# Six of the seven down products on scaled fp16 halves instead of fp32r halves

## The chip, the cores and the metric

The kernel runs on one core of one Trainium2 chip. The metric is the device time of one execution in microseconds (us). The five engines are TensorE (PE; its weight loads are listed apart as PEld), VectorE (DVE), ScalarE (ACT), GpSimd (POOL) and SyncE (SP, which here only issues DMAs).

## What is computed

Two layers of an encoder on 1024 tokens of width 1024. Each layer has an attention and a convolution branch, an output product, and a gated feed-forward block. The change lies in the second half of that block. Cut to it, the reference is:

```python
h2 = _rmsnorm(x, g_ffn[l])
z = _dwconv(h2 @ w_up[l], w_dw_ffn[l], b_dw_ffn[l])     # 1024 -> 2 * 2816, three taps along the tokens
zg, zv = jnp.split(z, 2, axis=-1)
x = x + (jax.nn.silu(zg) * zv) @ w_down[l]              # 2816 -> 1024, the "down" product
```

All inputs and the output are fp32. w_down has 22 blocks of 128 rows per layer.

## The kernel before

**Split operands.** TensorE multiplies fp32 numbers as a sum of two parts, hi and lo. ScalarE writes hi (a rounding copy), VectorE writes lo (source minus hi), and each product of two tiles is three matmuls: hi*hi, hi*lo, lo*hi. In the up products the parts are fp16, of operands first scaled by a power of two (`upper`, `lower`, lines 1183 to 1187; ScalarE adds the squares of each weight block, line 1130, one small matmul with ones sums them over the partitions, line 1163, and a few tiny VectorE operations make the exponent, lines 1132 to 1140). In the down products the parts are fp32r, unscaled (`pair`, lines 1616 to 1622).

**Seven products.** Up and down products are done by Strassen's scheme on two by two blocks: seven half-size products instead of eight. In the down stage (`down_steps`, line 1355) the halves are those of the 22 row blocks (j and j + 11), of the tokens (`done` = 0:512, `rest` = 512:1024) and of the output columns. The seven products run in `ORDER` = 1, 5, 6, 3, 7, 2, 4. Each has 11 steps j, a step is four output tiles m by three matmuls (`product`, line 1420), so 12 matmuls of 128x128 by 128x512. The sums of weight blocks that the scheme wants for products 5, 6, 3 and 7 are made during the up stage (`sum_load`, `sum_step`, `sum_store`, lines 1276 to 1288) and kept in DRAM; products 1, 2 and 4 read w_down itself. Sums of activations are made by VectorE in place (`combine`, line 1400). Eight PSUM banks form two sets of four: products 1, 6, 7, 4 accumulate in set 0 one on top of the other, 5 and 3 in set 1, 2 again in set 1. After each product VectorE adds the bank into x (`evict`, line 1444).

**The order of work.** `feed` (line 926) makes a list of TensorE steps: the output product, 154 up steps, 77 down steps. `put(step, rank, f)` hangs everything else behind a step; within a step, ranks decide. Each engine then runs its own instructions in exactly this order, and semaphores join the engines. For down step n: the weight rows are fetched by SP at n - 8 (`fetch`, pairs of j, into the three "wr" slots) and split at n - 4 (`turn`); `combine` stands at n - 3 (products 5, 6, 7), `pair`, the split of the activations, at n - 2 (eight "m" slots); evictions stand at the next product's first step. Products 2 and 4 (`DOWN_ADDED`) get their weights in another way: GpSimd's DMA queue loads and rounds hi (`cast`, line 1383), ScalarE writes its negative, and a second, adding DMA makes lo (`complete`, line 198).

**Ends.** In layer 0 the last three j of product 4 are done tile by tile (m outermost). In layer 1 it is the last six, and there in two column halves (`ENDS`): 144 matmuls of 128x256 in eight steps of 18, between which the final normalisation starts (lines 1557 to 1566).

**Around it.** Block f of the activations is finished by `close` (line 1264) in the up stage; blocks below 18 are stored to DRAM (`act_store`) and loaded back, 18 to 21 stay in SBUF. The 31 slots tagged "b" hold 128x1024 tiles of all kinds.

Of the kernel before, what the change touches and what calls it, by code (L numbers as in the profile page):

```python
# [9 lines left out]
F32 = mybir.dt.float32  # L10
# [21 lines left out]
NF = DFF // 128  # L32
# [103 lines left out]
class Encoder:  # L136
# [959 lines left out]
    def up_steps(self, l, steps, put):  # L1096
# [5 lines left out]
        self.kept = {}  # L1102
        raw, wts, zs, st, sums, scale, back, nback = defaultdict(dict), {}, defaultdict(dict), {}, {}, {}, {}, {}
        sub = lambda o, p, q, op=ALU.subtract: nc.vector.tensor_tensor(out=o, in0=p, in1=q, op=op)

# [158 lines left out]
        def close(f):  # L1264
# [5 lines left out]
            st["act", f] = z["v"]  # L1270

        def act_store(f):
            if f < KEPT:
                nc.sync.dma_start(out=self.actd[l][f], in_=st.pop(("act", f)))

        def sum_load(j):
            sums[j] = [self.blk(f"sd{l}_{j}{e}") for e in range(2)]
            for e, t in enumerate(sums[j]):
                nc.sync.dma_start(out=t, in_=a["w_down"][l, j + e * (NF // 2)])

        def sum_step(j, n):
# [73 lines left out]
    def down_steps(self, l, steps, put):  # L1355
        nc, a = self.nc, self.a
        base, last, half = len(steps), l == DEPTH - 1, NF // 2
        done, rest = HALVES
        act, x, casts, w, pairs, ps, nxt, sq, late_r, turns = {}, {}, {}, {}, {}, {}, {}, {}, {}, {}
        sub = lambda o, p, q, op=ALU.subtract: nc.vector.tensor_tensor(out=o, in0=p, in1=q, op=op)  # L1360
        spare = lambda name: self.pp.tile([128, 512], F32, name=name, tag="d4", bufs=1)
        other = lambda name: self.pp.tile([128, 512], F32, name=name, tag="d5", bufs=1)
# [19 lines left out]

        def cast(i, j):
            casts[i, j] = self.cast_pair(source(i, j, 1)[:, 0], f"wd{l}_{i}{j}", "wr" if j % 4 == 3 else "ws")

        def fetch(i, j):
            n = min(2, half - j)
            t = self.tmp("wr", f"wd{l}_{i}{j}r", F32, (128, 2, 512))
            nc.sync.dma_start(out=t[:, 0:n], in_=source(i, j, n))
            for k in range(n):  # L1390
                casts[i, j + k] = t[:, k]
# [21 lines left out]
        def pair(i, j):  # L1413
            src = {1: (j, rest), 5: (j, rest), 6: (j, rest), 3: (half + j, done), 7: (j, done), 2: (half + j, rest),
                   4: (half + j, rest)}[i]
            pairs[i, j] = self.pair(act[src[0]][:, src[1]], f"ab{l}_{i}{j}", "b" if i == 4 else "m")
            if i == 4:
# [16 lines left out]
        def evict_end(c, m):  # L1434
            xm = x[4 + m][:, ENDS[c]]
            sub(xm, xm, ps[BANK_SET[4], m][:, cols[c]])
            sq[c, m] = self.blk(f"xsq{l}_e{c}{m}")[:, 0:256]
# [16 lines left out]
        for i, j in order:  # L1454
# [10 lines left out]
            late = max(0, j - tail - 3) if i == 4 else 0  # L1465
            if i in DOWN_ADDED:
                put(need - 7 + late, 5, lambda i=i, j=j: cast(i, j))
            elif j % 2 == 0:
                put(need - 8, 5, lambda i=i, j=j: fetch(i, j))
            put(need - 4 + late - late // 2, 4, lambda i=i, j=j: turn(i, j))  # L1470
            if i in (5, 6, 7):
                put(need - 3, 3, lambda i=i, j=j: combine(i, j))
            put(need - 2, 3, lambda i=i, j=j: pair(i, j))
            if i == 2:
                put(need - 1, 3.5, lambda j=j: combine(4, j))
        for m in range(3, 4 if not last else 3):
            steps.append(lambda m=m: [product(4, j, (m,)) for j in range(tail, half)])
# [586 lines left out]
```

## Time and profile before

| | us |
|---|---|
| median of three runs | 2242.82 (2242.24 to 2243.37) |
| the profiled execution, its own time | 2243.32 |
| its span, first to last instruction | 2241.4 |
| TensorE busy in the span | 2228.5 |
| VectorE, ScalarE, GpSimd busy | 1806.3, 1360.0, 655.3 |
| up products, first to last start, layer 0 | 506.2 to 908 |
| down products, first to last start, layer 0 | 908.6 to 1119 |
| down products, first to last start, layer 1 | 2018 to 2231.6 |

Views of the profile used below: the page; groups of instructions by line and shape (busy time, mean ns of one, idle time before and what ended it); the timeline of an engine (start, length, line, output and input, count of merged instructions, idle time before in brackets). Neighbouring instructions of an engine overlap in part, so the distance of two starts is often a little less than the length of one.

### The profile page before, as it was taken

To read this page: it belongs to the slowest core of one execution; us is meant where nothing else is said; L and a number is where in the kernel's file an instruction comes from. 1 tells how busy PE (TensorE), PEld (TensorE's weight loads), DVE (VectorE), ACT (ScalarE), POOL (GpSimd) and SP (SyncE) were. 2 spreads that over 40 slices of the span, in tenths; PEclk is the share of its full clock that TensorE was granted. 3 is DMA by queue.
4 is the path that set the end of the run, shared out by engine and by line. 5 is a ranking of instruction groups with operands and counts; after the bars stand their busy time and mean duration, and the time that the engine had idled before them with its cause. 6 is when DMAs were issued, how large, how long until landed. Compare 5 with 4: busy or idle time off the path is not lost.

```text
span 2241.4 us, 30140 instructions
## 1 busy us (share of the span) xinstructions
PE 2228.5 (99%) x10762; PEld 1511.7 (67%) x10762; DVE 1806.3 (81%) x2484; ACT 1360.0 (61%) x2078; POOL 655.3 (29%) x631
## 2 busy tenths in 40 slices
PE   9999999999999999999999999999999999999998
PEld 8887777784444444788888877777744444448887
DVE  6989888768998887876559798887798988878765
ACT  5355977745766666544533568776467666655444
POOL 1222788511121111002412237964111121110032
PEclk9999999999999999999999999999999999999999
DMA  6888988955589896646968999979645888856466
GB/s 192 166 181 274 198 188 183 275 139 120 130 230 266 220 261 149 209 156 196 207 140 168 206 265 203 189 164 245 165 104 135 252 261 226 248 154 234 143 150 170
DMA packets 176965, 434.80 MB, mean 194 GB/s; under 512 B 24768, under 2 KB 32816, under 8 KB 176816
## 3 DMA queue, kind: packets, MB, share of 16 engines
q0 software_dynamic: 79520, 176.31, 41.4%
q1 hardware_dynamic: 97008, 256.04, 34.0%
q8 instruction: 85, 1.39, 0.3%
q10 hardware_dynamic: 288, 0.53, 0.1%
q14 instruction: 64, 0.52, 0.1%
HBM read 293.56 MB, written 80.40 MB: 167 GB/s over the span
## 4 chain that ended last, share of the span: by engine, by line
PE 94%; DMA 3%; DVE 1%; ACT 1%; issue 0%; SPq 0%; POOL 0%; DVEq 0%; POOLq 0%; ACTq 0%
PE p L1223 36%; PE pd L1426 19%; PE po L958 7%; PE s L1686 7%; PE o L1749 4%; PE t L1726 4%; PE pq L236 3%; PE pa L236 3%; PE pkv L236 2%; PE pg L236 2%; PE pg L554 2%; DMA wo<-in_w_o 1%; PE pk L236 1%; PE pa L554 1%; PE pn L236 1%; PE pv L1662 1%
## 5 line engine op out<-in xcount | busy, mean ns | idle before, releaser
L1223 PE MATMUL p<-b,w 128*128 128x512 f16 x3696 | 803.6, 379 | 0.0
L1223 PEld LDWEIGHTS <-w 128*128 128x128 f16 x3696 | 361.7, 99 | 426.9 <-DVE w L1187 0.6
L1426 PE MATMUL pd<-ab,wd 128*128 128x512 f32 (+1 forms) x1920 | 422.7, 382 | 0.0
L1426 PEld LDWEIGHTS pd<-ab,wd 128*128 128x128 f32 x1920 | 350.7, 188 | 69.7 <-DVE ab L1621 0.4
L1114 POOL DMA_DIRECT2D wu<-in_w_up x176 | 152.8, 882 | 745.4 <-DVE w L1187 520.7
L1686 PE MATMUL s<-k,q 96*128 96x512 f32 x768 | 207.7, 406 | 1.0 <-DVE qn L750 1.0
L1729 DVE SCALAR_TENSOR_TENSOR pt<-t,pt 128x512 f16<-128x512 f32 x256 | 164.8, 684 | 40.5 <-ACT pt L1728 39.9
L1187 DVE SCALAR_TENSOR_TENSOR w<-wu,wf,w 128x512 f16<-128x512 f32 (+1 forms) x216 | 177.0, 833 | 4.0 <-ACT w L1184 4.0
L1728 ACT ACTIVATE pt<-t 128x512 f16<-128x512 f32 x256 | 139.2, 596 | 57.6 <-PE t L1726 56.6
L1918 POOL TENSOR_TENSOR late<-gate,par 128x1016 f32<-128x1016 f32 (+11 forms) x78 | 168.9, 2166 | 13.8 <-PE pn L236 13.8
L1184 ACT ACTIVATE w<-wu,wf 128x512 f16<-128x512 f32 (+1 forms) x216 | 162.0, 781 | 0.2 <-DMA wu<-in_w_up 0.2
L1688 DVE TENSOR_REDUCE mx<-s 128x1 f32<-128x1024 f32 x128 | 155.6, 1216 | 0.0
L1686 PEld LDWEIGHTS s<-k,q 96*128 96x128 f32 x768 | 135.2, 189 | 23.9 <-DVE qn L750 1.4
L1901 DVE SCALAR_TENSOR_TENSOR conv<-gate,par,conv 128x1009 f32<-128x1009 f32 (+7 forms) x112 | 142.3, 1274 | 3.7 <-ACT conv L616 1.0
L1696 ACT ACTIVATE p<-s,mx 128x1024 f32<-128x1024 f32 x128 | 143.4, 1120 | 2.1 <-DVE mx L1688 1.7
L1619 ACT CAST ab<-ac 128x512 fp32r<-128x512 f32 x130 | 80.0, 616 | 102.5 <-DVE ac L1360 65.1
L1726 PEld LDWEIGHTS t<-ident,p 128*128 128x128 f32 x1024 | 119.7, 141 | 25.9 <-ACT p L1696 0.8
L1627 ACT ACTIVATE o<-zg,par 128x1024 f32<-128x1024 f32 x44 | 54.5, 1238 | 135.1 <-DVE zg L1231 135.1
L1726 PE MATMUL t<-ident,p 128*128 128x128 f32 x1024 | 133.7, 273 | 0.4 <-ACT p L1696 0.2
L1749 PE MATMUL o<-pt,v 128*128 128x512 f16 x512 | 132.5, 381 | 1.2 <-DVE pt L1729 1.1
L920 POOL DMA_DIRECT2D wd<-in_w_down x44 | 32.9, 751 | 322.2 <-PE pd L1426 321.2
L1633 DVE SCALAR_TENSOR_TENSOR o<-zg,par,o 128x1023 f32<-128x1023 f32 x88 | 112.6, 1280 | 8.0 <-ACT o L1627 6.5
(2114 smaller groups left out, 3871.4 us busy)
## 6 DMA issues: line engine op xcount, KB each, us to landing
wu<-in_w_up SPq DMA_DIRECT2D x98, 512.0 KB, 4.8
wu<-in_w_up POOLq DMA_DIRECT2D x176, 256.0 KB, 4.8
sd<-in_w_down SPq DMA_DIRECT2D x44, 512.0 KB, 5.0
ws<-sd SPq DMA_DIRECT2D x44, 512.0 KB, 8.1
wd<-in_w_down POOLq DMA_DIRECT2D x88, 256.0 KB, 5.6
act<-v SPq DMA_DIRECT2D x36, 512.0 KB, 7.3
ac<-act SPq DMA_DIRECT2D x72, 256.0 KB, 5.0
wo<-in_w_o POOLq DMA_DIRECT2D x64, 256.0 KB, 7.6
```

What stands on the lines that cost most here:

```text
L236: nc.tensor.matmul(ps[:, HALVES[c]], w, x[:, HALVES[c]], start=(k == 0 and s == 0), stop=(k == n - 1 and s == 2))
L958: self.nc.tensor.matmul(ps, p[:, sl], q[:, cs], start=(k == 0 and t == 0), stop=(k == 3 and t == 2))
L1184: nc.scalar.activation(out=t, in_=src, func=AF.Copy, scale=scale[f])
L1187: nc.vector.scalar_tensor_tensor(out=t, in0=src, scalar=scale[f], in1=hi, op0=ALU.mult, op1=ALU.subtract)
L1223: nc.tensor.matmul(ps, w[p][:, k * 128:(k + 1) * 128], b[:, q], start=(i in (1, 5, 2) and k == 0 and t == 0), stop=(k == 3 and t == 2), sk ...
L1426: nc.tensor.matmul(ps[t, m][:, cs], w[i, j][p][:, m * 128:(m + 1) * 128], b[:, q, cs], start=(i in (1, 5, 2) and j == 0 and s == 0), stop= ...
L1686: nc.tensor.matmul(ps[:, cs], q[i][0:96, qs], k[j][0:96, cs], start=(s == 0), stop=(s == 2))
L1688: nc.vector.tensor_reduce(out=mx, in_=ps, op=ALU.max, axis=AX.X, negate=True)
L1726: nc.tensor.transpose(tp[:, i, qi * 128:(qi + 1) * 128], st["p"][2 * qp + qi][:, kt * 128:(kt + 1) * 128], self.ident)
L1729: nc.vector.scalar_tensor_tensor(out=lo, in0=tp, scalar=P_SCALE, in1=hi, op0=ALU.mult, op1=ALU.subtract)
L1749: nc.tensor.matmul(po, v[2 * c + i][:, h // 2, e, :], pt[s][:, 2 * (c % 2) + i, :], start=(c == 0 and i == 0 and s == 0), stop=(c == 3 and ...
L1918: self.nc.gpsimd.tensor_tensor(out=p[:, lo:hi], in0=u[:, lo + s:hi + s], in1=self.tap(l, j, t).broadcast_to([128, hi - lo]), op=ALU.mult)
```

## The change

The first product (i = 1) stays as it was. The other six use fp16 parts of scaled operands, with one scale for all activations and one for all w_down of a layer.

- The scales come from sums of squares: 22 ScalarE squares of the closed activation blocks and 22 of the w_down blocks, all in the up stage; one matmul with ones behind down step 6; eight tiny VectorE operations (`scales`).
- Weights of products 2 and 4 are now fetched raw by SP as those of the others; `cast` and `complete` go out of the down stage. For the six products `turn` splits the rows of two j at once.
- Evictions multiply by the inverse scale. Set 0 holds product 1 unscaled when product 6 adds to it, so its four banks are multiplied in place (`rescale`).
- The loads for the weight sums come one step earlier; four activation stores come later; the last pairs of layer 1 come up to three steps earlier.

```diff
+SQUARE_LAG = {0: 5, 1: 7, 4: 5, 2: 5}
-DOWN_ADDED = (2, 4)
+DOWN_TOTAL = 6
...
+        self.ds = self.cp.tile([128, 2 * NF], F32, name=f"ds{l}", tag="ds", bufs=1)
+        def act_squares(f):
+            t = self.kept[f] if f >= KEPT else st["act", f]
+            nc.scalar.activation(out=self.blk(f"asq{l}_{f}", F16), in_=t, func=AF.Square, accum_out=self.ds[:, f:f + 1])
+        def sum_squares(j, e):
+            f = NF + j + e * (NF // 2)
+            nc.scalar.activation(out=self.blk(f"dsq{l}_{j}{e}", F16), in_=sums[j][e], func=AF.Square, accum_out=self.ds[:, f:f + 1])
...
-            put(max(m + 3, n + 5) + STORE_LAG, 3, lambda f=f: act_store(f))
+            c = max(m + 3, n + 5)
+            put(c + SQUARE_LAG.get(f, 1), 2.6, lambda f=f: act_squares(f))
+            put(c + max(STORE_LAG, SQUARE_LAG.get(f, 1)), 3, lambda f=f: act_store(f))
         for j in range(NF // 2):
             n = at[1, 7 + j * 13 // 11]
-            put(n - 4, 5, lambda j=j: sum_load(j))
+            put(n - 5, 5, lambda j=j: sum_load(j))
+            for e in range(2):
+                put(n - 2 + e, 2.4, lambda j=j, e=e: sum_squares(j, e))
...
+        plus = lambda o, p, by: nc.vector.scalar_tensor_tensor(out=o, in0=p, scalar=by, in1=o, op0=ALU.mult, op1=ALU.add)
         def turn(i, j):
-            if i in DOWN_ADDED:
-                w[i, j] = self.complete(*casts.pop((i, j)))
-            else:
-                t = self.pair(casts.pop((i, j)), f"wd{l}_{i}{j}", "ws")
+            raw = casts[i, j - j % 2]
+            if i == 1:
+                t = self.pair(raw[:, j % 2], f"wd{l}_{i}{j}", "ws")
                 w[i, j] = t[:, 0], t[:, 1]
+            elif j % 2 == 0:
+                n = min(2, half - j)
+                t = self.tmp("ws", f"wd{l}_{i}{j}", F16, (128, 2, 2, 512))
+                nc.scalar.activation(out=t[:, 0:n, 0], in_=raw, func=AF.Copy, scale=st["w"])
+                nc.vector.scalar_tensor_tensor(out=t[:, 0:n, 1], in0=raw, scalar=st["w"], in1=t[:, 0:n, 0], op0=ALU.mult, op1=ALU.subtract)
+                for k in range(n):
+                    w[i, j + k] = t[:, k, 0], t[:, k, 1]
+        def total():
+            st["ps"] = self.pp.tile([128, 2 * NF], F32, name=f"ds{l}p", tag="d4", bufs=1)
+            nc.tensor.matmul(st["ps"], self.ones, self.ds[:, 0:2 * NF], start=True, stop=True)
+        def scales():
+            f = self.ds[:, 0:16]
+            cut = lambda i, n=1: f[:, i:i + n]
+            nc.vector.tensor_reduce(out=cut(0, 2), in_=st.pop("ps").rearrange("p (e f) -> p e f", e=2), op=ALU.add, axis=AX.X)
+            nc.vector.tensor_scalar(out=cut(0, 2), in0=cut(0, 2), scalar1=2.0 ** -60, scalar2=None, op0=ALU.max)
+            self.half_exponent(cut(2, 2), cut(0, 2))
+            self.power(cut(4, 2), cut(2, 2), -1.0, 204.0)
+            self.power(cut(6, 2), cut(2, 2), 1.0, 50.0)
+            nc.vector.tensor_tensor(out=cut(8), in0=cut(4), in1=cut(5), op=ALU.mult)
+            nc.vector.tensor_tensor(out=cut(9), in0=cut(6), in1=cut(7), op=ALU.mult)
+            nc.vector.tensor_scalar(out=cut(10), in0=cut(9), scalar1=-1.0, scalar2=None, op0=ALU.mult)
+            st["a"], st["w"], st["up"], st["back"], st["nback"] = (cut(i) for i in (4, 5, 8, 9, 10))
+        def rescale(m):
+            p = ps[BANK_SET[1], m]
+            nc.vector.tensor_scalar(out=p, in0=p, scalar1=st["up"], scalar2=None, op0=ALU.mult)
...
         def pair(i, j):
...
+            if i == 1:
+                pairs[i, j] = self.pair(raw, name, tag)
+            else:
+                t = pairs[i, j] = self.tmp(tag, name, F16, (128, 2, 512))
+                nc.scalar.activation(out=t[:, 0], in_=raw, func=AF.Copy, scale=st["a"])
+                nc.vector.scalar_tensor_tensor(out=t[:, 1], in0=raw, scalar=st["a"], in1=t[:, 0], op0=ALU.mult, op1=ALU.subtract)
...
         def evict(i, m):
...
-            sub(xm, xm, ps[BANK_SET[i], m], ALU.subtract if o else ALU.add)
+            if i == 1:
+                sub(xm, xm, ps[BANK_SET[i], m], ALU.add)
+            else:
+                plus(xm, ps[BANK_SET[i], m], st["nback" if o else "back"])
...
-            if i in DOWN_ADDED:
-                put(need - 7 + late, 5, lambda i=i, j=j: cast(i, j))
-            elif j % 2 == 0:
-                put(need - 8, 5, lambda i=i, j=j: fetch(i, j))
+            if j % 2 == 0:
+                put(need - 8 + late, 5, lambda i=i, j=j: fetch(i, j))
...
-            put(need - 2, 3, lambda i=i, j=j: pair(i, j))
+            put(need - 5 + (j - tail) // 2 if i == 4 and last and j >= tail else need - 2, 3, lambda i=i, j=j: pair(i, j))
...
+        put(base + DOWN_TOTAL, 0.3, total)
+        put(base + DOWN_TOTAL, 0.6, scales)
+        for m in range(4):
+            put(at[1, half - 1] + 2 + m // 2, 2, lambda m=m: rescale(m))
```

More of the change, by code (lines that the diff above doesn't have):

```diff
@@ L1358, in down_steps @@
         done, rest = HALVES
-        act, x, casts, w, pairs, ps, nxt, sq, late_r, turns = {}, {}, {}, {}, {}, {}, {}, {}, {}, {}
+        act, x, casts, w, pairs, ps, nxt, sq, late_r, turns, st = {}, {}, {}, {}, {}, {}, {}, {}, {}, {}, {}
         sub = lambda o, p, q, op=ALU.subtract: nc.vector.tensor_tensor(out=o, in0=p, in1=q, op=op)
+        plus = lambda o, p, by: nc.vector.scalar_tensor_tensor(out=o, in0=p, scalar=by, in1=o, op0=ALU.mult, op1=ALU.add)
         spare = lambda name: self.pp.tile([128, 512], F32, name=name, tag="d4", bufs=1)
@@ L1381, in source @@
             return src[:, :, HALVES[c]].rearrange("j p c -> p j c")
-        def cast(i, j):
-            casts[i, j] = self.cast_pair(source(i, j, 1)[:, 0], f"wd{l}_{i}{j}", "wr" if j % 4 == 3 else "ws")
         def fetch(i, j):
@@ L1389, in fetch @@
             nc.sync.dma_start(out=t[:, 0:n], in_=source(i, j, n))
-            for k in range(n):
-                casts[i, j + k] = t[:, k]
+            casts[i, j] = t[:, 0:n]
         def turn(i, j):
-            if i in DOWN_ADDED:
-                w[i, j] = self.complete(*casts.pop((i, j)))
-            else:
-                t = self.pair(casts.pop((i, j)), f"wd{l}_{i}{j}", "ws")
+            raw = casts[i, j - j % 2]
+            if i == 1:
+                t = self.pair(raw[:, j % 2], f"wd{l}_{i}{j}", "ws")
                 w[i, j] = t[:, 0], t[:, 1]
+            elif j % 2 == 0:
[23 more added lines that the diff above has]
+            nc.vector.tensor_scalar(out=p, in0=p, scalar1=st["up"], scalar2=None, op0=ALU.mult)
         def combine(i, j):
@@ L1415, in pair @@
                    4: (half + j, rest)}[i]
-            pairs[i, j] = self.pair(act[src[0]][:, src[1]], f"ab{l}_{i}{j}", "b" if i == 4 else "m")
+            name, tag, raw = f"ab{l}_{i}{j}", "b" if i == 4 else "m", act[src[0]][:, src[1]]
+            if i == 1:
[4 more added lines that the diff above has]
+                nc.vector.scalar_tensor_tensor(out=t[:, 1], in0=raw, scalar=st["a"], in1=t[:, 0], op0=ALU.mult, op1=ALU.subtract)
             if i == 4:
@@ L1435, in evict_end @@
             xm = x[4 + m][:, ENDS[c]]
-            sub(xm, xm, ps[BANK_SET[4], m][:, cols[c]])
+            plus(xm, ps[BANK_SET[4], m][:, cols[c]], st["nback"])
             sq[c, m] = self.blk(f"xsq{l}_e{c}{m}")[:, 0:256]
```

## The prediction

> **What bounds the kernel now.** First the page: who is busy, and what TensorE does before and in the down stage.
>
> ```profile
> span 2241.4 us, 30140 instructions
> PE 2228.5 (99%) x10762; PEld 1511.7 (67%) x10762; DVE 1806.3 (81%) x2484; ACT 1360.0 (61%) x2078; POOL 655.3 (29%) x631
> ...
> L1223 PE MATMUL p<-b,w 128*128 128x512 f16 x3696 | 803.6, 379 | 0.0
> L1223 PEld LDWEIGHTS <-w 128*128 128x128 f16 x3696 | 361.7, 99 | 426.9 <-DVE w L1187 0.6
> L1426 PE MATMUL pd<-ab,wd 128*128 128x512 f32 (+1 forms) x1920 | 422.7, 382 | 0.0
> L1426 PEld LDWEIGHTS pd<-ab,wd 128*128 128x128 f32 x1920 | 350.7, 188 | 69.7 <-DVE ab L1621 0.4
> ```
>
> TensorE is 99% busy and never idle ahead of an up or a down matmul (0.0). Only the number of its matmuls or the time of each can shorten the kernel; for the other engines the question is whether they keep up. The change leaves the number alone. The mean of one (379, 382) covers overlap and hides the rate, so I take the rate from starts on TensorE's timeline: one block of the up stage between two scale sums, then layer 0's down products from the first to the next other instruction, then the end of layer 1.
>
> ```profile
> 752.42 0.28 PE L1163 MATMUL wt<-wf,ones_r 128*128 128x2 f32 x2
> 752.56 18.29 PE L1223 MATMUL p<-b,w 128*128 128x512 f16 x84
> 770.68 0.28 PE L1163 MATMUL wt<-wf,ones_r 128*128 128x2 f32 x2
> ```
>
> ```profile
> 908.59 81.77 PE L1426 MATMUL pd<-ab,wd 128*128 128x512 f32 x359
> ...
> 1093.79 0.60 PE L275 MATMUL rx_0t<-ident,xss 128*128 128x128 f32 x4
> ```
>
> ```profile
> 2209.81 16.47 PE L1426 MATMUL pd<-ab,wd 128*128 128x512 f32 x120
> 2226.11 0.50 PE L263 MATMUL rx_512p<-ones_r,xss 128*128 128x1 f32 x4
> ```
>
> fp16: 770.68 - 752.56 = 18.12 us for 84, **215.7 ns**. fp32r: 185.20 us; by the code these are 68 steps of 12, 816 matmuls (the trace lacks a few records), **227.0 ns**. The end: 16.30 us for 12 full ones (2.72) and 108 of half width, so 125.7 ns for a half.
>
> **Part 1, TensorE.** Of 2 x 924 full-width equivalents, product 1 keeps 264. There remain 1584: 72 of them are the 144 halves, 1512 are full. 1512 x 11.3 ns = 17.1 us. fp16 halves aren't in the trace: bounds are half of 215.7 (107.9 ns) and that plus fp32r's excess over its own half (125.7 - 113.5 = 12.2, so 120.1). I take 110, near the lower one, because the fp16 weight load (99 ns) fits beside such a matmul and fp32r's (188) doesn't. Only 126 of them count, the last 18 run beside VectorE's final chain: 126 x 15.7 = 2.0 us (0.7 to 2.2). Sum: **19.1 us** less.
>
> The Trainium skill's rule speaks against it: "TensorE: Matmul & The Clock Gate", section "Back-to-back issue gap", gives 518 cycles, about 216 ns, for 512 columns and names no element type. The fp16 rows agree (215.7), the fp32r rows don't (227.0); by that rule alone the sum of part 1 would be nil. It is a rival below.
>
> **Part 2, the scale sum on TensorE.** Two matmuls with 44 columns. The two-column one moves the next product by 0.14 us (752.42 to 752.56); four transposes of 128 fp32 columns last 0.60 together (1093.79). I take 0.3 each, nearer the first, which does the same with fewer columns: **0.6 us** more (0.3 to 1.2).
>
> **Part 3, the squares on ScalarE.** Rows by form, for this and the next parts, with the landing time of the sums' loads:
>
> ```profile
> L1187 DVE SCALAR_TENSOR_TENSOR w<-wu,wf,w 128x512 f16<-128x512 f32 x180 | 131.1, 745 | 2.6 <-ACT w L1184 2.6
> L1184 ACT ACTIVATE w<-wu,wf 128x512 f16<-128x512 f32 x180 | 124.4, 710 | 0.2 <-DMA wu<-in_w_up 0.2
> L1130 ACT ACTIVATE wsq<-wu 128x1024 f16<-128x1024 f32 x88 | 92.1, 1047 | 8.7 <-DMA wu<-in_w_up 8.7
> L1619 ACT CAST ab<-ac 128x512 fp32r<-128x512 f32 x130 | 80.0, 616 | 102.5 <-DVE ac L1360 65.1
> L1187 DVE SCALAR_TENSOR_TENSOR w<-wu,wf,w 128x1024 f16<-128x1024 f32 x36 | 45.9, 1276 | 1.3 <-ACT w L1184 1.3
> L1360 DVE TENSOR_TENSOR x<-x,pd 128x512 f32<-128x512 f32 x52 | 35.5, 687 | 77.2 <-PE pd L1426 77.2
> L1130 ACT ACTIVATION_READ_ACCUMULATOR wsq<-wu 128x1 f32 x88 | 16.8, 190 | 0.0
> sd<-in_w_down SPq DMA_DIRECT2D x44, 512.0 KB, 5.0
> ```
>
> A square with its read is 1047 + 190 ns, some 1.14 us from start to start. Per block of 18.3 us comes one of activations and, in 11 of the blocks 7 to 18, two of weights: 3.4 us. Steps and ranks put all three between the first split of the next block and `conv_start`. There ScalarE's timeline has its one large hole; VectorE's and SP's rows show what the squares need:
>
> ```profile
> 755.93 1.75 ACT L1184 ACTIVATE w<-wu,wf 128x1024 f16<-128x1024 f32 x2
> 761.31 1.24 ACT L1627 ACTIVATE o<-zg,par 128x1024 f32<-128x1024 f32 x1 [3.63 <-DVE zg L1231]
> 763.12 0.69 ACT L1230 ACTIVATE zv<-p,wf 128x512 f32<-128x512 f32 x1 [0.56 <-PE p L1223]
> ...
> 773.61 0.69 ACT L1230 ACTIVATE zv<-p,wf 128x512 f32<-128x512 f32 x1 [1.43 <-PE p L1223]
> ```
>
> ```profile
> 755.82 1.22 DVE L1104 TENSOR_TENSOR v<-v,o 128x1024 f32<-128x1024 f32 x1
> ```
>
> ```profile
> 753.78 0.90 SPq L1279 DMA_DIRECT2D sd<-in_w_down x2
> ```
>
> The hole is 3.63 us, the squares fill 3.4. `close` ends at 757.04, before its square is due. The weights' loads, issued at 753.78 and 5.0 us under way, would land at 758.8, in the hole already; the change moves them ahead. So I cost part 3 at **nothing**. Its cover is the hole and 2.0 us more of waits for TensorE (0.56, 1.43); behind a late square stand `conv_start`, the evictions and the next split, whose TensorE step lies two steps (5.2 us) away.
>
> **Part 4, the handover.** PE's scale sum waits for the square of block 21, the scales on VectorE for PE. VectorE's timeline there, and what tiny operations cost:
>
> ```profile
> 919.76 1.22 DVE L1104 TENSOR_TENSOR v<-v,o 128x1024 f32<-128x1024 f32 x1
> ...
> 936.90 2.73 DVE L1360 TENSOR_TENSOR x<-x,pd 128x512 f32<-128x512 f32 x4 [4.61 <-PE pd L1426]
> 939.55 0.69 DVE L1621 TENSOR_TENSOR ab<-ac,ab 128x512 fp32r<-128x512 f32 x1
> 940.15 0.69 DVE L1360 TENSOR_TENSOR ac<-ac 128x512 f32<-128x512 f32 x1
> 940.75 0.68 DVE L1621 TENSOR_TENSOR wd<-wd_54r,wd 128x512 fp32r<-128x512 f32 x1
> 941.58 0.69 DVE L1621 TENSOR_TENSOR ab<-ac,ab 128x512 fp32r<-128x512 f32 x1
> ```
>
> ```profile
> 753.28 0.15 DVE L1135 TENSOR_REDUCE wf<-wt 128x1 f32<-128x2 f32 x1
> 753.47 0.15 DVE L882 TENSOR_SCALAR wf<-wf 128x1 int32<-128x1 int32 x1
> ```
>
> Block 21 closes at 921.0, its square ends at 922.3. Step 6 ends at 908.59 + 84 x 0.227 = 927.7, so **TensorE doesn't wait** (5 us to spare). VectorE does: from about 924 it stands until 928.1, then eight operations 0.19 apart, 1.5 us, to 929.6. Queued behind them is lo of activation 8, done at 930.3; TensorE needs it at 930.6 + 0.2 (hi*hi goes first). It fits by half a microsecond. VectorE's former idle time of 4.61 us pays for this, and it comes to the evictions about 1 us late, where nothing waits. I cost it at 0.2 us a layer (0 to 1).
>
> **Part 5, VectorE in products 5, 6, 7.** Start to start, VectorE needs 0.60 for a combine or an eviction (939.55 to 940.15), 0.66 with a scale (745 against 687 ns), 1.2 for two rows of weights (1276), against 2 x 0.60 before. From a combine to its lo lie 1.43 us (940.15 to 941.58), with the scaled hi 0.09 more (710 against 616): 1.52. Two steps: lo 0.66, combine to lo 1.79 (0.60 + 1.19, weights between), lo 0.66, combine to lo 1.52: 4.63 us, of TensorE's 24 x 0.2157 = 5.18. Eleven steps 25.5 and four evictions 2.6 make 28.1 of 28.5. In product 5 `rescale` adds four operations on a bank; the nearest row is the eviction (687), so 2.4 us. In product 7 the sums of squares add 2.2 us:
>
> ```profile
> 1033.15 0.68 DVE L254 SCALAR_TENSOR_TENSOR xss<-xss,xsq 128x512 f32<-128x512 f32 x1
> 1033.94 1.49 DVE L256 TENSOR_TENSOR xss<-xss,xsq 128x512 f32<-128x512 f32 x2
> ```
>
> So VectorE falls 2 us behind there. It comes to the next eviction up to 1.1 us after the product's end instead of 1.7 before, finishes at +3.7 and the next lo at +4.4; the lead of two steps puts the need at +5.2. Product 3 has no combine and gives the time back. Product 2 and 4 gain 0.6 us of weights a step on VectorE and lose two DMAs on GpSimd's queue; product 2 then has 1.9 us of VectorE a step, of 2.59. Cost: nothing, covered by less than 1 us.
>
> **Part 6, the end of layer 1.** By the starts of part 5, VectorE has, from 1.7 us ahead of product 2's end to the long last step (15.4 us: 1.7, five steps of 2.59, two sets of transposes), evictions 2.6, nine splits 5.9, weights 4.2, a root 2.1 (a reduction of 0.7, seven tiny ones) and sums 2.2, together 17.0; only the sums may come late. In the column halves behind it it has this slack now, and TensorE's six steps ahead of that root shorten by 1.7:
>
> ```profile
> 2227.10 0.16 DVE L292 TENSOR_SCALAR rx_512y<-rx_512p 128x2 int32<-128x2 int32 x1 [2.44 <-PE rx_512p L266]
> ```
>
> I cost it at 1.1 us (0 to 3).
>
> **Sum.** -19.1 + 0.6 + 0.4 + 1.1 = **-17.0 us**. The profiled execution took 2243.3 us (1.9 more than its span), 0.5 over the median: 2226.3 for it, 2225.8 for the median. I say 2226.
>
> **The rivals.**
>
> *VectorE becomes the bound.* If its operations don't overlap as in the rows (full lengths: 5.06 us for two steps, 3.0 for evictions, 2.75 for the rescale), products 5 and 7 need 33.6 and 33.0 of 28.5 us; after the lead of some 3.5 and product 3's relief TensorE stands about 5 us a layer: 2236. For it: 28.1 of 28.5. Against: the overlaps are in the rows, and the same pattern held its rate in products before.
>
> *Slower: ScalarE delays the up stage.* The w_down squares stand ahead of `conv_start` in one queue. If their loads, or the slots these go into, come late by more than hole and waits hold (5.6 - 3.4 = 2.2 us past the hole) and the splits' lead of about 2.5 us, each of the 22 pairs stalls TensorE. From 0.8 us a pair the gain is gone; at 1.5 it costs 33 us: 2259. Against: the load lands inside the hole even where it is now.
>
> *The rate doesn't change.* If what costs fp32r 11 ns is the stage and not the type, only the costs stay: 2243.3 + 1.7 = 2245. This is also what the skill's one gap for all types would give. Against: projection products with fp32r elsewhere in the trace start some 225 ns apart too (82.66 to 83.11 for two), up products at the same clock 215.7.
>
> ```profile
> 82.66 0.61 PE L236 MATMUL pg<-xs_7h,wg30h 128*128 128x512 f32 x2
> 83.11 0.62 PE L236 MATMUL pg<-xs_7l,wg30h 128*128 128x512 f32 x2
> ```
>
> **Chances.** Forecast (2222.5 to 2230) 0.78; VectorE the bound (2230 to 2242) 0.10; ScalarE, slower, 0.07; no change of rate 0.05. The measurement can tell about 0.2%, 4.5 us. Faster by more: 0.78 and most of 0.10, 0.86; within: 0.07; slower: 0.07. Range: 2222.5 is all of 19.1, the halves at their lower bound and almost no stall; 2235 takes in half of the VectorE case.
>
> **What would show it.** Right: down matmuls of the six products 216 ns apart; TensorE's idle time ahead of L1426 under 3 us; VectorE idle only 1 us or less ahead of evictions of products 5 to 7; the hole ahead of `conv_start` gone, conv_start at its place. Wrong: idle time ahead of L1426 put down to lo (L1621's successor) in products 6, 3 or 2; ahead of L1223 put down to L1187; the scale sum waiting for ScalarE.

## The result and the profile after

The changed kernel takes **2224.88 us** in the median (2222.78 to 2227.56, four runs) against 2243.01 before (2242.24 to 2243.37, four runs): the ratio is **0.992** (95% interval 0.9903 to 0.9937). The profiled execution of the changed kernel is its longest, 2227.56 us with a span of 2225.6.

The page and its groups of TensorE instructions come first (busy time, mean ns of one, idle time before them):

```profile
span 2225.6 us, 30035 instructions
PE 2211.7 (99%) x10766; PEld 1373.5 (62%) x10766; DVE 1843.7 (83%) x2492; ACT 1461.9 (66%) x2194; POOL 592.2 (27%) x543
...
L1225 PE MATMUL p<-b,w 128*128 128x512 f16 x3696 | 804.0, 379 | 0.0
L1470 PE MATMUL pd<-ab,wd 128*128 128x512 f16 (+2 forms) x1920 | 404.2, 373 | 0.0
L1470 PEld LDWEIGHTS <-wd 128*128 128x128 f16 x1656 | 161.9, 98 | 179.3 <-issue 0.5
```

TensorE still never idles ahead of an up or a down matmul (0.0), ScalarE has 102 us more work and VectorE 37, and next to none of that is on the path (parts 3 and 5 of the prediction). The gain must then be in the time of one matmul. TensorE's timeline gives the corner points of both layers (the rows are those shown of before, with their counterparts of layer 1):

```profile
911.20 19.44 PE L1470 MATMUL pd<-ab,wd 128*128 128x512 f32 x84
930.48 0.31 PE L1419 MATMUL ds0p<-ds,ones_r 128*128 128x44 f32 x2
930.62 158.82 PE L1470 MATMUL pd<-ab,wd 128*128 128x512 f32 x732
1089.27 0.60 PE L276 MATMUL rx_0t<-ident,xss 128*128 128x128 f32 x4
...
1113.27 0.58 PE L549 MATMUL pg<-xs_0h,wg01h 128*128 128x512 f32 x1
```

```profile
2012.23 19.42 PE L1470 MATMUL pd<-ab,wd 128*128 128x512 f32 x84
...
2196.34 14.54 PE L1470 MATMUL pd<-ab,wd 128*128 128x512 f16 x120
2210.72 0.50 PE L264 MATMUL rx_512p<-ones_r,xss 128*128 128x1 f32 x4
```

A merged row is named by its first instruction: the 732 of "f32" are 48 of product 1 and 684 in fp16. From 930.62 to 1089.27 are 158.65 us; less 48 x 0.227 there remain 147.75 for 684, **216.0 ns** each. The end of layer 1: 14.38 us, less 12 x 0.2157, over 108 halves, **109.2 ns**. Of before, three points are still needed:

```profile
506.20 6.00 PE L1223 MATMUL p<-b,w 128*128 128x512 f16 x27
```

```profile
1119.22 0.39 PE L548 MATMUL pg<-xs_0h,wg01h 128*128 128x512 f32 x1
```

```profile
2018.35 185.36 PE L1426 MATMUL pd<-ab,wd 128*128 128x512 f32 x816
```

In the changed kernel the first up product starts at 508.64. The account by stage, in us:

| stage, by TensorE's starts | before | after | difference |
|---|---|---|---|
| start to the first up product | 506.20 | 508.64 | +2.44 |
| up products of layer 0 | 402.39 | 402.56 | +0.17 |
| down products of layer 0 | 210.63 | 202.07 | -8.56 |
| next layer, to its down products | 899.13 | 898.96 | -0.17 |
| down products of layer 1, to `rx_512p` | 207.76 | 198.49 | -9.27 |
| end | 15.29 | 14.88 | -0.41 |
| span | 2241.4 | 2225.6 | -15.8 |

The first row is none of the change's doing: the code ahead of the up products is the same in both, and a later execution of the changed kernel (experiment 10) reached its first up product at 506.39, with a span of 2223.3. In the execution above, the very first products of the program stood waiting for their operand:

```profile
7.48 0.79 PE L510 MATMUL pg<-xs_0h,wg00h 128*128 128x512 f32 x1 [1.05 <-ACT xs_0h L447]
```

So the change itself is worth **18.2 us**, 17.8 of it in the two down stages. The 0.4 of the end is not clearly the change's: kernels with all down products in fp32r took between 14.88 and 15.29 us there (15.29 before, 15.03, 14.88 and 14.92 in experiments 1, 2 and 7).

### The profile page after: what moved, and what is told of

It reads as the page before. It is cut to its first block, busy times and chain, and to the rows that moved or that the text cites. A ratio compares the mean times of both kernels' runs of the same rounds, so it can differ in the third digit from the quotient of the medians.

```text
span 2225.6 us, 30035 instructions
## 1 busy us (share of the span) xinstructions
PE 2211.7 (99%) x10766; PEld 1373.5 (62%) x10766; DVE 1843.7 (83%) x2492; ACT 1461.9 (66%) x2194; POOL 592.2 (27%) x543
## 4 chain that ended last, share of the span: by engine, by line
PE 89%; DVE 5%; DMA 3%; ACT 2%; issue 1%; POOL 0%; SPq 0%; DVEq 0%; POOLq 0%; ACTq 0%
PE p L1225 36%; PE pd L1470 17%; PE po L959 7%; PE s L1735 7%; PE o L1798 4%; PE t L1775 4%; PE pa L237 2%; PE pg L237 2%; DVE conv L1950 2%; PE pg L555 2%; PE pq L237 1%; PE pkv L237 1%; PE pa L555 1%; DMA wo<-in_w_o 1%; PE pn L237 1%
## 5 line engine op out<-in xcount | busy, mean ns | idle before, releaser
L1470 PE MATMUL pd<-ab,wd 128*128 128x512 f16 (+2 forms) x1920 | 404.2, 373 | 0.0
L1470 PEld LDWEIGHTS <-wd 128*128 128x128 f16 x1656 | 161.9, 98 | 179.3 <-issue 0.5
L1459 ACT ACTIVATE ab<-ac,ds 128x512 f16<-128x512 f32 x108 | 75.5, 717 | 108.6 <-DVE ac L1374 75.4
L1233 DVE SCALAR_TENSOR_TENSOR zg<-p,wf,zg 128x512 f32<-128x512 f32 x72 | 54.0, 750 | 71.4 <-PE p L1225 61.7
L1682 DVE SCALAR_TENSOR_TENSOR v<-zv,par,v 128x1023 f32<-128x1023 f32 x88 | 112.1, 1276 | 0.0
```

Source lines behind the costliest of these rows:

```text
L1470: nc.tensor.matmul(ps[t, m][:, cs], w[i, j][p][:, m * 128:(m + 1) * 128], b[:, q, cs], start=(i in (1, 5, 2) and j == 0 and s == 0), stop= ...
L1682: self.nc.vector.scalar_tensor_tensor(out=o[:, a:b], in0=z[:, at + a:at + b], scalar=self.par[l][:, tap:tap + 1], in1=o[:, a:b], op0=ALU.m ...
```

## The experiments

**1. The parts scaled, but fp32r.** Everything of the change stays, except that the six products multiply fp32r parts (the split then writes one weight row at a time).

```diff
-                t = self.tmp("ws", f"wd{l}_{i}{j}", F16, (128, 2, 2, 512))
+                t = self.tmp("ws", f"wd{l}_{i}{j}", F32R, (128, 2, 512))
...
-                t = pairs[i, j] = self.tmp(tag, name, F16, (128, 2, 512))
+                t = pairs[i, j] = self.tmp(tag, name, F32R, (128, 2, 512))
```

> The changed kernel with one thing taken back: the scaled parts of the six products are fp32r instead of fp16 (one row of weights a split, as before). Squares, scale sum, rescale, raw rows by SP all stay. Theory (the gain is the distance of two matmuls, 227.0 against 215.7 ns, and nothing else): 1512 full matmuls and 126 halves give it all back, about 19 us, so 2243 to 2245, ratio to the kernel before 0.999 to 1.002, and 227 ns between starts in the six products. Rival (the gain comes from the raw rows and the lighter GpSimd queue): it stays near 2225.

Measured: 2244.8 us against 2242.94, ratio 1.0004 (0.9995 to 1.0013). The whole gain is gone. On TensorE's timeline the six products are back at 166.06 us for 732, 226.9 ns:

```profile
929.74 166.22 PE L1468 MATMUL pd<-ab,wd 128*128 128x512 f32 x732
1095.80 0.60 PE L276 MATMUL rx_0t<-ident,xss 128*128 128x128 f32 x4
```

What follows: the element type is the gain, but for about 0.5 us; squares, scales, scaled evictions and raw rows together cost at most some 2 us. The 0.5 us lie at the end of layer 1, where the 120 products ahead of `rx_512p` take 15.79 us here (2211.68 to 2227.47) against 16.30 before. Of before, the timeline of the weight loads shows two of them standing for VectorE's lo there, 0.18 us at 2214.38 and 0.19 at 2214.98; here none stands. The likely reason is that the change makes these last pairs earlier; that alone was not tried.

**2. Only the raw rows.** The kernel before, with the weights of products 2 and 4 fetched by SP and split on chip, in fp32r.

```diff
-DOWN_ADDED = (2, 4)
+DOWN_ADDED = ()
...
-            if i in DOWN_ADDED:
-                put(need - 7 + late, 5, lambda i=i, j=j: cast(i, j))
-            elif j % 2 == 0:
-                put(need - 8, 5, lambda i=i, j=j: fetch(i, j))
+            if j % 2 == 0:
+                put(need - 8 + late, 5, lambda i=i, j=j: fetch(i, j))
```

> The kernel before with only the fetching of products 2 and 4 changed: raw rows by SP and a split on ScalarE and VectorE, all parts fp32r and unscaled. Theory: GpSimd's queue was not on TensorE's path, so within 2 us of 2243 (ratio 0.999 to 1.001). Rival (part of the gain is the queue's): 5 us faster or more.

Measured: 2241.7 us, ratio 0.9999 (0.999 to 1.0009). GpSimd is busy 63 us less, as in the changed kernel, and it is worth nothing.

**3. Fixed scales.** The changed kernel without the 44 squares a layer and without the scale sum; the scales are set to 1. That computation is left out.

```diff
-            put(c + SQUARE_LAG.get(f, 1), 2.6, lambda f=f: act_squares(f))
...
-                put(n - 2 + e, 2.4, lambda j=j, e=e: sum_squares(j, e))
...
-            nc.vector.tensor_reduce(out=cut(0, 2), in_=st.pop("ps").rearrange("p (e f) -> p e f", e=2), op=ALU.add, axis=AX.X)
...
+            nc.vector.memset(cut(0, 10), 1.0)
+            nc.vector.memset(cut(10), -1.0)
...
-        put(base + DOWN_TOTAL, 0.3, total)
```

> The changed kernel without its 44 squares a layer and without the scale sum; the scales are the constant one (that part of the computation is left out). Theory (ScalarE's squares lie in its idle hole, the sum costs TensorE 0.14 us a layer, VectorE's wait is covered): 0 to 1 us faster than the changed kernel, 2223.5 to 2225.5, ratio about 0.992. Rival (the squares cost something in the up stage): 3 us faster than the changed kernel or more, under 2222.

Measured: 2225.58 us, ratio 0.9923 (0.9908 to 0.9938), no less than the changed kernel. The medians can't tell less than about a microsecond, but the stages can: from the first up product to `rx_512p` TensorE needs 1701.21 us here, against 1702.08 and 1702.00 in the two profiles of the changed kernel. So parts 2 to 4 of the prediction cost 0.8 to 0.9 us together, about 0.17 in each up stage and 0.26 in each down stage.

**4. Product 1 in fp16 too.** It gets scales of its own from the blocks that are closed ten steps ahead of the down stage (11 weight blocks and 11 activation blocks), and `rescale` multiplies by the ratio.

```diff
+        put(base - 10, 0.3, total1)
+        put(base - 10, 0.6, scales1)
```

> The changed kernel with product 1 in fp16 too, on scales of its own operands (the squares of activation blocks 0 to 10 and weight blocks 0 to 10, summed ten steps ahead of the down stage); its banks are then multiplied by the ratio of the two scales. Theory: 264 matmuls by 11.3 ns are 3.0 us, a second scale sum costs 0.14 a layer: 2.7 us faster than the changed kernel, 2222, ratio 0.9905 to 0.991. Rival (VectorE is too dense at the handover, the steps of product 1 are 0.13 us shorter and its splits longer): TensorE waits there and the gain is under 1 us or a loss.

Measured: 2224.55 us, ratio 0.9917 (0.99 to 0.9933), 0.3 under the changed kernel's median. Each down stage is 1.8 us shorter, but each up stage takes 404.06 us instead of 402.56, so most of the gain was lost ahead of the down stage. First TensorE's timeline, then VectorE's:

```profile
885.90 0.29 PE L1435 MATMUL dt0p<-ds,ones_r 128*128 128x22 f32 x2
886.04 2.75 PE L1225 MATMUL p<-b,w 128*128 128x512 f16 x12
889.80 20.88 PE L1225 MATMUL p<-b,w 128*128 128x512 f16 x96 [1.01 <-DVE zv L1233]
```

```profile
886.23 0.18 DVE L1440 TENSOR_REDUCE dt<-dt0p 128x2 f32<-128x22 f32 x1 [3.38 <-PE dt0p L1435]
...
889.00 0.74 DVE L1233 SCALAR_TENSOR_TENSOR zv<-p,wf,zv 128x512 f32<-128x512 f32 x1
```

VectorE came to its reduction 3.38 us ahead of TensorE's sum and stood. A split, a `close` and the eviction of a bank (889.00) were queued behind it, and TensorE waited 1.01 us for that bank. Each engine runs its own instructions in the program's order, so a wait for TensorE placed right behind TensorE's own step made VectorE stand for as long as it was ahead, and everything queued behind was late.

**5. Every new square twice.** The second writes the same values.

```diff
-            nc.scalar.activation(out=self.blk(f"asq{l}_{f}", F16), in_=t, func=AF.Square, accum_out=self.ds[:, f:f + 1])
+            o = self.blk(f"asq{l}_{f}", F16)
+            for _ in range(2):
+                nc.scalar.activation(out=o, in_=t, func=AF.Square, accum_out=self.ds[:, f:f + 1])
```

> The changed kernel with each of its 44 new squares a layer done twice, one right behind the other, into the same place. Theory (they fill ScalarE's hole of 3.63 us a block, with 2.0 us of later waits and two steps of lead behind it): 6.8 us a block overrun hole and waits by 1.2 us in 22 blocks; VectorE's waits for ScalarE take it up and TensorE loses at most 1 us in some blocks: 0 to 10 us slower than the changed kernel, 2225 to 2235. Rival (there is no such cover, a late square stops TensorE at once): each block loses the whole 3.4 us, 75 us or more, over 2290.

Measured: 2247.34 us, ratio 1.002 (1.001 to 1.0029): 22.5 us over the changed kernel, between the two expectations, so both missed. The group of up products, then TensorE's timeline in layer 0:

```profile
L1225 PE MATMUL p<-b,w 128*128 128x512 f16 x3696 | 811.3, 380 | 13.1 <-ACT zg L1232 11.8
```

```profile
628.42 13.11 PE L1225 MATMUL p<-b,w 128*128 128x512 f16 x60 [1.13 <-ACT zg L1232]
646.29 3.90 PE L1225 MATMUL p<-b,w 128*128 128x512 f16 x11 [4.76 <-ACT zg L1232]
```

TensorE's waits for ScalarE's evictions that this view counts lie in one place per layer, 5.9 us, and not in each block (what the other blocks lose is the subject of experiment 9). That place is where the first activation blocks are closed, one soon after the other, and where `SQUARE_LAG` puts their squares. In the changed kernel ScalarE has no room there. In the view by windows of the changed kernel the columns are the window and its length, then PE, PEld, DVE, ACT, POOL (busy us and count), TensorE's granted clock, DMA share and GB/s:

```profile
630.00:635.00 5.00, 5.00 (x24) 2.24 (x23) 5.00 (x6) 5.00 (x8) 0.87 (x1) 1.00 1.00 292
...
640.00:645.00 5.00, 5.00 (x25) 2.25 (x23) 5.00 (x7) 5.00 (x9) 0.87 (x1) 1.00 1.03 308
645.00:650.00 5.00, 5.00 (x26) 2.48 (x25) 4.93 (x11) 4.33 (x7) 0.00 (x0) 1.00 0.75 184
```

From 625 to 650 ScalarE is busy for 24.1 of 25 us and runs six of the new squares. At 1.04 us from the start of one to the next instruction, doubling them adds 6.2 us where 0.9 is free. The same view of the doubled kernel:

```profile
640.00:645.00 5.00, 1.53 (x8) 0.59 (x6) 1.52 (x2) 4.97 (x10) 0.00 (x0) 1.00 0.66 179
645.00:650.00 5.00, 3.71 (x11) 1.41 (x11) 5.00 (x7) 5.00 (x9) 0.87 (x1) 0.66 0.17 27
```

The 0.66 is a mean over a window in which the wait ends (646.29). By windows of half a microsecond the granted clock is 0.68 from 645.5, 0.50 from 646.0 to 649.0, 0.91 in the next and 1.00 again from 649.5. The twelve products behind the wait take 3.95 us, to the scale sum at 650.24, where 12 x 0.2157 is 2.59: so the wait was paid a second time in part. The up stages took 412.2 and 413.3 us instead of 402.6.

**6. Every second lo twice.** In products 5, 6 and 7, lo of the activations of odd j is written twice, 15 operations more a layer on VectorE.

```diff
+                for _ in range(2 if i in (5, 6, 7) and j % 2 else 1):
+                    nc.vector.scalar_tensor_tensor(out=t[:, 1], in0=raw, scalar=st["a"], in1=t[:, 0], op0=ALU.mult, op1=ALU.subtract)
```

> The changed kernel with lo of the activations of every odd j written twice in products 5, 6 and 7 (15 more VectorE operations of 0.66 us a layer). Theory (VectorE is within a microsecond or two of bounding these products): 28.1 us become 31.4, with the rescale 33.8 and with the sums of squares 33.6, of TensorE's 28.5; after the lead of some 3 us TensorE stands 5 us in products 5 and 6 and 2 us in product 7 of each layer: 8 to 20 us slower than the changed kernel, 2233 to 2245. Rival (VectorE has more room than it seems): under 3 us slower.

Measured: 2233.89 us, ratio 0.9965 (0.9952 to 0.9978), 9.0 over the changed kernel. By stages, where the start of the program doesn't count, the two down stages take 3.9 and 3.6 us longer: of 15 x 0.67 = 10 us added to VectorE in each layer, less than half came through. On TensorE's timeline its waits for lo begin in product 5 and grow in product 6:

```profile
954.05 5.34 PE L1471 MATMUL pd<-ab,wd 128*128 128x512 f16 x24 [0.30 <-DVE ab L1461]
959.81 15.91 PE L1471 MATMUL pd<-ab,wd 128*128 128x512 f16 x72 [0.42 <-DVE ab L1461]
976.87 2.75 PE L1471 MATMUL pd<-ab,wd 128*128 128x512 f16 x12 [1.15 <-DVE ab L1461]
```

VectorE is near the bound in these products but not at it: some 6 us a layer were still free.

**7. Narrower fp32r.** The kernel before, run once; product 3 has 64 columns of weights (half of its output rows are left out), product 7 is cut into two halves of 256 tokens.

```diff
+                k = 64 if i == 3 else 128
...
+                    for c in (slice(0, 256), slice(256, 512)) if i == 7 else (cs,):
+                        nc.tensor.matmul(ps[t, m][0:k, c], w[i, j][p][:, m * 128:m * 128 + k], b[:, q, c],
```

> The kernel before, all fp32r, with product 3 on 64 of the 128 weight columns of each tile (half of its output rows are left out) and product 7 with each matmul cut into two of 256 columns. The rate of each product is read from starts. Theory (the fp32r matmul itself has a longer fixed part): product 3 stays at 227 ns a matmul, product 7 takes 125 ns a half. Rival (fp32r's weight load, 188 ns for 128 columns, is what holds the matmul up): with 64 columns the load is about half and product 3 falls to 216 ns.

Measured: 2249.05 us, span 2247.1. Evictions on VectorE's timeline, each waiting for TensorE, mark the ends of products 6, 3 and 7; then the two kinds of weight loads by form:

```profile
998.02 2.73 DVE L1360 TENSOR_TENSOR x<-x,pd 128x512 f32<-128x512 f32 x4 [7.28 <-PE pd L1428]
1028.35 2.76 DVE L1360 TENSOR_TENSOR x<-x,pd 128x512 f32<-128x512 f32 x4 [7.57 <-PE pd L1428]
...
1059.94 2.85 DVE L1360 TENSOR_TENSOR x<-x,pd 128x512 f32<-128x512 f32 x4 [6.14 <-PE pd L1428]
```

```profile
L1428 PEld LDWEIGHTS pd<-ab,wd 128*128 128x128 f32 x1920 | 315.0, 189 | 49.3 <-DVE ab L1623 0.4
...
L1428 PEld LDWEIGHTS pd<-ab,wd 128*64 128x64 f32 x264 | 35.4, 134 | 25.2
```

Product 3: 30.33 us for 132 matmuls, 229.8 ns, with a weight load of 134 ns instead of 189 (the kernel before has the same two evictions 29.92 us apart, 226.7 ns). A shorter load doesn't bring the fp16 rate. Product 7: 31.59 us for 264, 119.7 ns, less than its own weight load lasts; so the load's length in the records is not a floor for the distance. The 125.7 ns that the prediction took for a half at the end of layer 1 contain the two waits named under experiment 1; in that experiment, where they are gone, the same halves are 121.0 ns apart (15.79 us less 12 x 0.227, over 108). Two widths give a line: fp32r 0.419 ns a column and **12.4 ns** fixed (227.0, 119.7), fp16 0.416 a column and **2.7 ns** (215.7, 109.2). The columns cost the same in both; fp32r has about 10 ns more for each matmul. Where that comes from stays open.

**8. Experiment 4 with its sums ahead of their readers.**

```diff
-        put(base - 10, 0.3, total1)
-        put(base - 10, 0.6, scales1)
+        put(base - 11, 0.3, total1)
+        put(base - 9, 0.6, scales1)
...
-        put(base + DOWN_TOTAL, 0.6, scales)
+        put(base + DOWN_TOTAL + 1, 0.6, scales)
```

> All seven products in fp16 as in the run with product 1 in fp16, but each scale sum stands one step or more ahead of the VectorE operations that read it (first sum 11 steps ahead of the down stage and its scales 9, second scales one step behind their sum), so that VectorE does not stand waiting for TensorE. Theory (the earlier version lost 1.6 us in the up stage because VectorE, waiting for the first sum, was late with an eviction): that comes back, no idle time of TensorE ahead of up matmuls, 2.7 us faster than the changed kernel, 2222, ratio 0.990 to 0.991. Rival (VectorE is too dense there anyway): as the earlier version, 0.9917.

Measured: 2222.68 us, ratio 0.9914 (0.9899 to 0.9929). The waits ahead of the down stage are gone, the up stage takes 402.9 us instead of experiment 4's 404.1: the cause of that loss is shown. Of the 0.3 us that it still takes over the changed kernel's 402.6, 0.14 are the added sum.

**9 and 10. Only the later squares twice, and the changed kernel again.** Squares of blocks below 8 and of the first weight pair stay single, so the dense place keeps its load. Both on one chip.

```diff
+            for _ in range(2 if f >= 8 else 1):
...
+            for _ in range(2 if j >= 1 else 1):
```

> The changed kernel with squares done twice only from activation block 8 and from the second pair of weight blocks on; the first, which fall together some 120 to 140 us into the up stage, stay single. With all squares twice TensorE's wait of 4.8 us lay in that one place. Theory (the cover per block was judged rightly for the steady part and wrongly for the bunch of the first closings): the later doubles cost TensorE almost nothing, within 2 us of the changed kernel, 2223 to 2227. Rival (the steady blocks pay too): 5 us slower or more.

> The changed kernel again, beside the next run on the same chip. Theory: as before, 2224 to 2226, ratio 0.991 to 0.993.

Measured: 2230.74 us (ratio 0.9944, 0.9931 to 0.9958) against 2225.37 for the changed kernel (0.9924, 0.9912 to 0.9937). I had expected less than 2 us for the difference of 5.4, and the rival, that the steady blocks pay too, 5 or more; by stages it is 3.6, so the steady blocks do pay. In the two profiled executions (spans 2228.8 and 2223.3) 1.66 us of the difference is the start-up of the program (508.05 and 506.39 at the first up product); the up stages give 1.8 each. There TensorE's timeline shows no wait, but a steady block takes 18.35 us from its first product to the next scale sum, where the changed kernel takes 18.13 (698.12 to 716.25). The timelines of the weight loads and of ScalarE show where it goes:

```profile
700.01 18.51 PE L1225 MATMUL p<-b,w 128*128 128x512 f16 x84
718.36 0.28 PE L1165 MATMUL wt<-wf,ones_r 128*128 128x2 f32 x2
```

```profile
715.78 2.25 PEld L1225 LDWEIGHTS <-w 128*128 128x128 f16 x11 [0.34 <-issue]
```

```profile
715.06 0.67 ACT L1232 ACTIVATE zg<-p,wf 128x512 f32<-128x512 f32 x1
```

The weight loads stand 0.34 us and go on at 715.78, when ScalarE's eviction of a bank has just ended (715.73). Eight blocks of each layer have such a gap, of 0.34 or 0.35 us, and each of the eight in layer 0 ends 0.05 or 0.06 us behind that eviction. The changed kernel has none in these blocks, and there the same eviction ends 13.84 us behind the block's first product (711.96) instead of 15.72. So the view shows no releaser, but the times say that TensorE waited for ScalarE. The doubled squares cost 0.22 us in each of eight blocks, 1.8 a layer, and the dense place makes up most of experiment 5's loss: of the 9.7 and 10.7 us by which its up stages are longer, some 2 are steady blocks.

**11. Experiment 8 again, on the same chip as 9 and 10.**

> All seven products in fp16 with each scale sum ahead of its readers, again, beside the changed kernel on the same chip. Theory (264 matmuls by 11.3 ns, two more scale sums of 0.14): 2.7 us faster than the changed kernel. Rival (the end of the run takes it back, as 0.8 us of it were in the first look): 2 us or less.

Measured: 2223.58 us (2222.7 to 2225.55), ratio 0.9916 (0.9903 to 0.993), 1.8 us under the changed kernel's 2225.37 (2224.36 to 2227.87). The ranges and the intervals overlap, so the times alone don't separate the two. The profiles do: from the first up product to `rx_512p` TensorE needs 2205.48 - 506.35 = 1699.13 us, and 2208.39 - 506.39 = 1702.00 in the changed kernel. Of these 2.9 us, 0.9 comes back at the very end. There the stores of the output land later. Issues by DMA queue, first of the changed kernel in experiment 10, then of this one (KB each, median us from issue to landing):

```profile
out_y<-x SPq DMA_DIRECT2D x8, 128.0 KB, 1.8
```

```profile
out_y<-x SPq DMA_DIRECT2D x8, 128.0 KB, 3.8
```

Why they land later was not tried.

## Why the prediction was right, point by point

The forecast was 2226.0, the median is 2224.88, inside the range of 2222.5 to 2235. The change proper is -18.2 us by stages (-18.1 between the medians) where the sum said -17.0. The mechanism is the one forecast. That the medians agree to 1.1 us is in part luck: the start of the program alone moves a single execution by more than 2 us, and a gain taken too large (part 1) stands against costs taken too large (parts 4 and 6).

- **Part 1, the rate: right, and 0.7 us too large.** 19.1 was expected. The two down stages are 8.56 + 9.27 = 17.83 us shorter with the scale sums, 0.27 each, in them, so 18.4; by rates, 1512 x 11.0 ns and 108 x 16.5 ns, it is 18.4 as well. Of the 16.5, 4.7 are not the type's, but the two waits of before at the end of layer 1 (experiment 1), 0.5 us in all. The halves took 109.2 ns where I took 110. The reason given for the halves was wrong, though: that the 188 ns load does not fit beside an fp32r half can't be what sets its rate, since experiment 7 has such matmuls 119.7 ns apart.
- **Part 2, the scale sums: right.** 0.27 us each, 0.3 were forecast. From 930.48 to 930.62 only 0.14 of it shows; the rest is behind the sum, where the second product starts 0.31 us after the first. From the first down product to the first weight load of the next product it is 30.43 us (911.20 to 941.63), and 30.16 in experiment 3 without the sum (909.23 to 939.39). In experiment 8, where the products around the sum are fp16, it costs 0.15: 909.26 to 927.53 are 18.27 us, and 84 x 0.2157 is 18.12.
- **Part 3, the squares: almost nothing.** The up stage takes 402.56 us, without squares 402.38 (experiment 3), so 0.17 to 0.18 a layer where nothing was forecast. In the steady block ScalarE's timeline shows the hole filled and `conv_start` in its place; a square takes 1.04 us from start to start, not 1.14:

```profile
759.58 1.04 ACT L1289 ACTIVATE dsq<-sd 128x1024 f16<-128x1024 f32 x1
...
760.62 1.04 ACT L1276 ACTIVATE asq<-v 128x1024 f16<-128x1024 f32 x1
...
762.27 1.04 ACT L1289 ACTIVATE dsq<-sd 128x1024 f16<-128x1024 f32 x1
...
763.93 1.24 ACT L1676 ACTIVATE o<-zg,par 128x1024 f32<-128x1024 f32 x1 [0.52 <-DVE zg L1233]
```

  The idle time ahead of `conv_start` went from 3.63 to 0.52. The margin was judged on this one steady block, however. The first closings, around 625 to 650, have 0.9 us of room in 25, and the prediction did not look there. The 0.17 us are lost in that stretch: the weight loads stand 0.29 us ahead of 629.89, and without the squares they don't. The "slower" rival named the right engine and the wrong place: not the loads of the weights in each pair, but mostly that bunch, would decide it (experiments 5 and 9).
- **Part 4, the handover: right.** On VectorE's timeline it stood 4.22 us for the scale sum (4 were forecast), and no matmul waited:

```profile
925.92 0.69 DVE L1670 TENSOR_TENSOR wd<-wd_18r,wd 128x512 fp32r<-128x512 f32 x1
930.83 0.20 DVE L1424 TENSOR_REDUCE ds<-ds0p 128x2 f32<-128x44 f32 x1 [4.22 <-PE ds0p L1419]
...
932.01 0.69 DVE L1670 TENSOR_TENSOR ab<-ac,ab 128x512 fp32r<-128x512 f32 x1
```

  The eight tiny operations took 1.2 us, not 1.5. The wait did no harm only because nothing but one split was urgent behind it; experiment 4 has the same pattern sixteen steps earlier, with an eviction behind it, and there it cost 1 us a layer.
- **Part 5, VectorE: right in the result, and pessimistic.** Still the same timeline, at the end of product 5, whose last matmul starts at 969.9 and makes way for the next one 0.2 us later, at 970.1; then the evictions behind product 7:

```profile
945.75 1.41 DVE L1436 TENSOR_SCALAR pd<-pd,ds 128x512 f32<-128x512 f32 x2
...
969.91 2.72 DVE L1375 SCALAR_TENSOR_TENSOR x<-pd,ds,x 128x512 f32<-128x512 f32 x4
972.55 0.74 DVE L1460 SCALAR_TENSOR_TENSOR ab<-ac,ds,ab 128x512 f16<-128x512 f32 x1
...
1053.86 2.73 DVE L1375 SCALAR_TENSOR_TENSOR x<-pd,ds,x 128x512 f32<-128x512 f32 x4 [2.01 <-PE pd L1470]
```

  Two `rescale` take 1.41 us, 0.7 each (0.6 forecast). Behind product 5 the evictions begin 0.2 us ahead of the product's end (1.1 behind it was allowed), the next lo is done at +3.2 (+4.4 forecast, +5.2 needed). In products 6 and 7 VectorE is early: it stands 2.25 and 2.01 us before it can evict, where the prediction had it 2 us behind in product 7 and named 1 us of idle time or less as a sign of being right. So the cover was larger than "less than 1 us"; experiment 6 shows that it is limited, since of 10 us more a layer less than 4 reached TensorE.
- **Part 6, the end:** 1.1 us were taken, none came. VectorE's wait for `rx_512p` shrank from 2.44 to 1.12 and did not vanish:

```profile
2211.71 0.16 DVE L293 TENSOR_SCALAR rx_512y<-rx_512p 128x2 int32<-128x2 int32 x1 [1.12 <-PE rx_512p L267]
```

- **The rival "the rate doesn't change"** is refuted by experiment 1 from the other side: with everything but the type the time is that of before. So the gap that the Trainium skill gives without naming a type ("TensorE: Matmul & The Clock Gate", section "Back-to-back issue gap", there called the isolated one: 518 cycles for 512 columns, 262 for 256) holds here for fp16, 215.7 ns at 512 columns and 109.2 at 256, and not for fp32r, 227.0 and 119.7.

Parts 2 to 4 together were taken at 1.0 us and cost 0.8 to 0.9, though not where they were put: part 3 cost something and part 4 nothing that shows. Part 6, taken at 1.1, cost nothing. It is the largest single error in the sum.

## What to carry to other kernels

Take a matmul's price from the distance of starts on a long, unbroken stretch, not from the mean length of a group: 379 and 382 ns on the page were 215.7 and 227.0 by distance, and nearly the whole gain lay in that. Judge room on an engine at its densest place, not in a typical block, since one crowded stretch of 25 us made up most of what more ScalarE work cost. Where an engine reads a result of TensorE in the middle of its queue, place the reader a step or two behind the sum, and look at what is queued behind it.

## What the runs showed of the hardware

- fp32r matmuls cost the same per column as fp16 ones and about 10 ns more each, at 512 columns and at 256; halving the weight columns shortened the load (189 to 134 ns) and did not bring the fp16 rate (229.8 ns against 215.7).
- A wait of 4.76 us on TensorE was followed by a granted clock of 0.50 for about three microseconds (646.0 to 649.0, experiment 5). After the wait of 1.01 us in experiment 4 the products kept their rate (889.80 to 910.52 for 96, 215.8 ns).
- The start of the program differs by more than 2 us between executions with the same code ahead of the up products (506.39 and 508.64 at the first up product in two profiles of the changed kernel), which is as much as several of the effects looked for. Stage by stage comparison takes it out, medians of a few runs may not.
- A wait can be missing from TensorE's own timeline: in experiment 9 eight blocks a layer lost 0.22 us each, and only the weight loads show the gap, 0.34 us, which ends 0.05 us behind ScalarE's eviction.
- A small fp32 sum between products cost more than the distance to the next start: 0.27 us among fp32r products, of which 0.14 show ahead of the next product, and 0.15 among fp16 ones (experiment 8).
